# Tile-major residual stream with 16 KB load rows, and rope tables packed as 4 KB rows, in an eight-core diffusion backbone

## The chip, the cores and the metric

One Trainium2 chip, eight cores. Each core computes one sample of the batch; nothing is exchanged between them. The metric is the device time of the slowest core, in microseconds. The kernels fell into a slower state in some executions. In one of the kernel before (3697.43 us), the cores of one die took 3677 to 3696 us at a granted TensorE clock of 0.86 to 0.87, those of the other 3379 to 3394 us at 0.97.

Most fast runs of one kernel agree within about 0.2% (3392.45 to 3398.03 us in nine runs of the kernel before, in one call), and this study is about effects of 0.2 to 0.3%.

## The reference, cut to what matters

Four layers on a stream `x` of 2048 tokens by 1024 channels, with 256 context tokens beside it. Layer 0 begins like this:

```python
mod = silu_c @ w_mod[l] + b_mod[l]                       # shift, scale, gate
hx = modulate(rms_norm(x, norm1_g[l]), sh1, sc1)          # needs x and the modulation
px = hx @ w_in                                            # pooling channels, q, k, v
q = axial_rope(q, ang_r, ang_c); k = axial_rope(k, ang_r, ang_c)
...                                                       # window attention, pooling, MLP
```

The stream is kept transposed: channels on the 128 partitions (8 chunks of 128), tokens along the free dimension, in five tiles: four of 512 latent tokens and one of 256 context tokens.

## The kernel before: the parts that matter

The stream `X` stays in SBUF for the whole run. It is loaded once, tile by tile, on the SyncE queue. In HBM a tile is already one contiguous block of 16 KB for each partition. In SBUF it is chunk-major (all tokens of a chunk lie together, so the eight chunks of one tile lie apart), and the load moves 128 x 8 rows of 2 KB:

```python
X = SB("X", [128, 8, NT], F32)                            # NT = 2304 tokens
def load_x(tile, after=()):
    (t0, n, s, ti) = tile
    Sd.dma("sp", Sd.chan("x%d" % ti), X[:, :, t0:t0 + n],
           xP[:, 8 * t0:8 * (t0 + n)].rearrange("p (c t) -> p c t", c=8), reads=after, writes=xk(ti))
```

`after` names weight slabs: X tile 1 is issued when the third `w_mod` slab has landed, tiles 2 to 4 when the fourth has. Between them the SyncE queue issues the rope tables, two DMAs of 2 KB rows for each tile.

Weights come on another queue, that of GpSimd, which casts float32 in HBM to bfloat16 in SBUF: a slab of 128 rows, 16 KB read and 8 KB written each (`w_kv` is half as wide: 8 KB read and 4 KB written). In the trace their packets have the size written: 8192 and 4096 B. There are four slots. The queue's order at the start is: four `w_mod` slabs, three small constants, then `w_kv`, `w_q`, `w_u` as slots come free, then more `w_mod` slabs:

```python
mods = [get_slab(w_mod[0, j], 8) for j in range(4)]
Sd.dma("pool", Sd.chan("ident"), IDB[:, :], identd, ...)          # rows of 64 B
first_mixer = even_mixer(0, X5, [... load_x(X5[i + 1], [mods[min(i + 2, 3)][1]]) ...])
#   in even_mixer:  permc (rows of 256 B), masks (rows of 512 B) on the GpSimd queue;
#                   for i in range(4): load_rope(i, i); loads[i]()      on the SyncE queue
for j in range(4):
    mod_slab(0, j, mods[j])                                       # then the norm of tile 0, piece by piece
...
kvs = get_slab(w_kv[i2], 8); qs_ = get_slab(w_q[i2], 8); us_ = get_slab(w_u[i2], 8)
kv_tile(all5[0], kvs, rope_buf(0), 1)                             # first K and V matmuls
```

After these three slabs are placed, one slot is left, and the remaining `w_mod` slabs of layer 0 pass through it one after the other. The sixth slab (the second to go through that slot) is issued once the fifth has been used, so the moment when the load of the sixth `w_mod` slab is issued marks how far the start has come; it is my stage mark.

The softmax here doesn't subtract the row's maximum and nothing guards it: scores larger than these inputs give would overflow.

Of the kernel before, what the change touches and what calls it, by code (L numbers as in the profile page):

```python
# [6 lines left out]
F32 = mybir.dt.float32  # L7
BF16 = mybir.dt.bfloat16
ALU = mybir.AluOpType
AF = mybir.ActivationFunctionType  # L10
# [4 lines left out]
NT = S + L  # L15
# [226 lines left out]
def build():  # L242
# [3 lines left out]
    def din(name, shape):  # L246
        dt_in[name] = nc.dram_tensor(name, list(shape), F32, kind="ExternalInput").ap()
        return dt_in[name]
# [14 lines left out]
    identd = din("ident", [128, 32])  # L263
    bandsd = din("bands", [128, 20 * 128])
    masksd = din("masks", [128, 2 * 128])
    ropec = din("ropec", [128, NT])
    ropes = din("ropes", [128, NT])
    permd = din("permc", [128, 128])
    outP = nc.dram_tensor("outP", [128, 8 * S], F32, kind="ExternalOutput").ap()
    gscr = nc.dram_tensor("gscr", [D, GW], BF16).ap()  # L270
# [1 line left out]
    with ExitStack() as st:  # L272
        def SB(name, shape, dt):
            return st.enter_context(nc.sbuf_tensor(name, shape, dt))

        X = SB("X", [128, 8, NT], F32)
        H = SB("H", [128, 8, NT], BF16)
        WR = [SB("wr%d" % i, [128, 4096], BF16) for i in range(NSLOT)]
        nvec = sum(n for _, n in VEC_LAYOUT)
# [21 lines left out]
        def vec(nm, a, b):  # L301
            return VEC[:, voff[nm] + a: voff[nm] + b]

        def emit(Sd, plan):
            dry = Sd.dry
            A = Arena(ART, ARENA_W, Sd)
            psk = lambda i: ("ps", i)
            hk = lambda ti: [("H", ti, c) for c in range(8)]
            xk = lambda ti: [("X", ti, c) for c in range(8)]

            def ACT(out, in_, func, reads, writes, **kw):
                Sd.op("act", "activation", (out, in_, func), kw, reads, writes)
# [4 lines left out]
            def STT(out, in0, scalar, in1, op0, op1, reads, writes):  # L317
                Sd.op("dve", "scalar_tensor_tensor", (out, in0, scalar, in1, op0, op1), None, reads, writes)
# [65 lines left out]
            ACT(SC[:, :], vec("cvec", 0, 16), AF.Silu, VK, [("c", "sc")])  # L384
            def load_x(tile, after=()):
                (t0, n, s, ti) = tile
                Sd.dma("sp", Sd.chan("x%d" % ti), X[:, :, t0:t0 + n], xP[:, 8 * t0:8 * (t0 + n)].rearrange("p (c t) -> p c t", c=8),
                       reads=after, writes=xk(ti))

            def zero_pads():  # L390
# [30 lines left out]
            def gate(which, c, s):  # L421
                o_ = ((3 * which + 2) * 8 + c) * 2 + s
                return MODV2[cur["lb"]][:, o_:o_ + 1]
# [3 lines left out]

            def norm_sq(tile, c, k=2):
                (t0, n, s, ti) = tile
                ACT(H[:, c:c + k, t0:t0 + n], X[:, c:c + k, t0:t0 + n], AF.Square, [("X", ti, q) for q in range(c, c + k)],  # L430
                    [("H", ti, q) for q in range(c, c + k)])

            def norm_stats(tile, r, pb=None):
# [10 lines left out]
            def norm_piece(lb, nrm, tile, r, c, mode="da"):  # L444
                (t0, n, s, ti) = tile
                tb = c % 2
                rst, rk, ak = RST[:, r, 0:n], ("rst", r), ("ab", lb, nrm, c // 2)
                tmp, x, h = TMP[:, tb, 0:n], X[:, c, t0:t0 + n], H[:, c, t0:t0 + n]
                if mode == "da":
                    STT(tmp, x, abv(lb, nrm, 0, c, s), rst, ALU.mult, ALU.mult, [("X", ti, c), rk, ak], [("tmp", tb)])  # L450
                    ACT(h, tmp, AF.Identity, [("tmp", tb), ak], [("H", ti, c)], bias=abv(lb, nrm, 1, c, s), scale=1.0)
                else:
                    if mode == "pd":
                        Sd.op("pool", "tensor_tensor", (tmp, x, rst, ALU.mult), None, [("X", ti, c), rk], [("tmp", tb)])
                    else:
                        TT(tmp, x, rst, ALU.mult, [("X", ti, c), rk], [("tmp", tb)])
                    DVE("tensor_scalar", (h, tmp, abv(lb, nrm, 0, c, s), abv(lb, nrm, 1, c, s), ALU.mult, ALU.add),
                        [("tmp", tb), ak], [("H", ti, c)])
# [14 lines left out]
            def push_final(tile, outb, sq=True):  # L473
                (t0, n, s, ti) = tile
                ob, ok = outb
                if sq:
                    for c in (0, 2, 4, 6):
                        push((lambda c_: (lambda: norm_sq(tile, c_)))(c))
                r = next_rst()
                push(lambda: norm_stats(tile, r))  # L480

                def piece(c):
                    STT(ob[:, c, 0:n], X[:, c, t0:t0 + n], vec("fing", c, c + 1), RST[:, r, 0:n], ALU.mult, ALU.mult,
                        [("X", ti, c), ("rst", r)] + VK, [ok[c]])
                    if c % 2:
                        Sd.dma("sp", Sd.chan("o%d%d" % (ti % 2, c // 2)), outP[:, 8 * t0 + (c - 1) * n:8 * t0 + (c + 1) * n].rearrange("p (c t) -> p c t", c=2),
                               ob[:, c - 1:c + 1, 0:n], reads=ok[c - 1:c + 1])
                for c in range(8):
                    push((lambda c_: (lambda: piece(c_)))(c))

            def mlp_phase(l, tiles, next_l, next_tiles):
# [24 lines left out]
                def stage2(w2s, it, last):  # L516
                    (t0, n, s, ti) = tiles[it]
                    hb, hbk = hid[it % 2]
                    for oc in range(8):
                        pb = dbank()  # L520
                        for kk in range(4):
                            MM(PS[pb][:, 0:n], w2s[0][:, kk, oc * 128:(oc + 1) * 128], hb[:, kk, 0:n], kk == 0, kk == 3,
                               reads=[w2s[1], hbk[kk]], writes=[psk(pb)], last=(kk == 3))
                        STT(X[:, oc, t0:t0 + n], PS[pb][:, 0:n], gate(1, oc, s), X[:, oc, t0:t0 + n], ALU.mult, ALU.add,
                            [psk(pb), gkey(1, oc), ("X", ti, oc)], [("X", ti, oc)])
                        if last and ti in next_ti and oc % 2:
                            norm_sq(tiles[it], oc - 1)
                        step()
                    if last and ti in next_ti:
                        if is_final:  # L530
                            push_final(tiles[it], outbs[it % 2], sq=False)
                        else:
                            push_norm(next_l % 2, 0, tiles[it], ("n1", ti), NORM1_MODE, sq=False)
# [19 lines left out]
            def proj_item(slabs_, tile, oc):  # L553
                (t0, n, s, ti) = tile
                pb = dbank()
                sl = slabs_[oc // 4]
                for k in range(8):
                    MM(PS[pb][:, 0:n], sl[0][:, k, (oc % 4) * 128:(oc % 4 + 1) * 128], H[:, k, t0:t0 + n], k == 0, k == 7,
                       reads=[sl[1], ("H", ti, k)], writes=[psk(pb)], last=(k == 7))
                STT(X[:, oc, t0:t0 + n], PS[pb][:, 0:n], gate(0, oc, s), X[:, oc, t0:t0 + n], ALU.mult, ALU.add,  # L560
                    [psk(pb), gkey(0, oc), ("X", ti, oc)], [("X", ti, oc)])

            def conv_mixer(l, tiles):
# [164 lines left out]
            def even_mixer(l, tiles, loads=()):  # L728
# [7 lines left out]
                V, Vk0 = A.bf16("V", 18, 128, parts=9)  # L736
                Qs = [A.bf16("Qs%d" % i, 4, 512, parts=4) for i in range(2)]
                Us = [A.bf16("Us%d" % i, 512) for i in range(NU_)]
                Pb = [A.bf16("P%d" % i, 1024) for i in range(NP)]
                Db = [A.bf16("Db%d" % i, 512) for i in range(2)]  # L740
                BND, Bk = A.bf16("BND", 20, 128)
                MSK, Mk = A.bf16("MSK", 2, 128)
                PW, PWk = A.bf16("PW", 4, 128)
                RT = [(A.f32("rc%d" % i, 512), A.f32("rs%d" % i, 512)) for i in range(2)]
                t1, t1k = A.f32("t1", 512)
                UB = [A.bf16("UB%d" % i, 512) for i in range(2)]
                PRM, PRk = A.bf16("PRM", 128)
# [8 lines left out]
                cur["nbank"] = 7  # L756

                def rope_buf(i):
                    if i < 2:
                        return RT[i]  # L760
                    return tuple((Pb[2 * i - 4 + j][0].bitcast(F32), Pb[2 * i - 4 + j][1]) for j in range(2))

                def load_rope(ti, i):
                    t0, n = all5[ti][0:2]
                    (rc, rck), (rs, rsk) = rope_buf(i)
                    Sd.dmas("sp", Sd.chan("rt%d" % i), [(rc[:, 0:n], ropec[:, t0:t0 + n]), (rs[:, 0:n], ropes[:, t0:t0 + n])], writes=rck + rsk)

                def rope_a(pq, tab, n):
                    (rc, rck), (rs, rsk) = tab
                    ub = UB[cnt["u"] % 2]  # L770
                    cnt["u"] += 1
                    TT(t1[:, 0:n], PS[pq][:, 0:n], rc[:, 0:n], ALU.mult, [psk(pq)] + rck, t1k)
                    TT(ub[0][:, 0:n], PS[pq][:, 0:n], rs[:, 0:n], ALU.mult, [psk(pq)] + rsk, ub[1])
                    return ub

                def rope_bc(ub, n, dst, dkeys):
# [312 lines left out]
def _prep_shared(inp):  # L1089
# [50 lines left out]
    sh["ident"] = ident  # L1140
    sh["bands"] = bands
    sh["masks"] = masks
    sh["ropec"] = rc
    sh["ropes"] = rs
    return {k: np.ascontiguousarray(v, dtype=np.float32) for k, v in sh.items()}, vecs

def run(inputs, cores=8):
# [21 lines left out]
```

## Time and profile before

| what | value | view |
|---|---|---|
| time, median of 3 runs | 3395.78 us (3393.93 to 3396.72) | runs |
| profiled run, slowest core | 3394.9 us | page |
| PE busy | 90% | page, part 1 |
| DMA's share of the chain of waits | 4% | page, part 4 |
| DMA share in the first four 20 us windows | 0.89, 1.01, 1.01, 0.99 | windows |

Part 4 of the page follows the work that ended last back to the start and says on which engine each share of the span was spent. Before:

```profile
PE 72%; DVE 13%; ACT 8%; DMA 4%; issue 2%; POOL 0%; SPq 0%; DVEq 0%; POOLq 0%; ACTq 0%
```

The kernel is bound by matmuls; loads hold it for 4% of the span, and a part of that lies at the start. The windows view of the start, with the length of a stretch, the busy us of PE, PEld, DVE, ACT and POOL in it (in brackets their instructions), then the granted clock, the mean busy share of the 16 DMA engines, and the GB/s that they wrote:

```profile
0.00:20.00 20.00, 0.99 (x32) 0.94 (x32) 0.75 (x6) 2.99 (x4) 4.60 (x12) 1.00 0.89 169
20.00:40.00 20.00, 1.24 (x33) 1.07 (x34) 0.50 (x3) 1.76 (x2) 0.53 (x1) 1.00 1.01 200
40.00:60.00 20.00, 13.37 (x115) 7.01 (x115) 10.30 (x21) 9.62 (x13) 0.53 (x1) 1.00 1.01 259
60.00:80.00 20.00, 13.47 (x67) 6.97 (x70) 10.59 (x17) 11.14 (x15) 0.00 (x0) 0.74 0.99 268
```

For 80 us the DMA engines have no pause, and PE is nearly idle for the first 40. The chain of waits in order of time names what it waits for (start, length, what):

```profile
2.75 29.76 DMA wr<-w_mod
32.53 24.18 DMA X<-xP
...
106.99 10.16 DMA wr<-w_mod
118.52 8.62 DMA wr<-w_mod
```

The DMA view of the first 130 us gives, for each load, its size and the time from issue to landing:

```profile
X<-xP SPq DMA_DIRECT2D x4, 2048.0 KB, 28.5
wr<-w_q POOLq DMA_DIRECT2D x1, 1024.0 KB, 27.0
wr<-w_kv POOLq DMA_DIRECT2D x1, 512.0 KB, 27.6
ARENA<-masks POOLq DMA_DIRECT2D x1, 64.0 KB, 38.1
ARENA<-permc POOLq DMA_DIRECT2D x1, 32.0 KB, 37.6
IDB<-ident POOLq DMA_DIRECT2D x1, 8.0 KB, 36.4
```

Even 8 KB take 36 us to land, because they stand in line behind four weight slabs: on the eight cores the first packet of the identity starts at 34.4 to 35.6 us. The timeline of PE shows the first K matmuls of the kernel, and what ended the idle time before them:

```profile
49.95 2.34 PE L144 MATMUL psa<-H,wr 128*128 128x512 bf16 x5 [0.24 <-issue]
53.09 1.03 PE L144 MATMUL psa<-H,wr 128*128 128x512 bf16 x2 [0.80 <-ACT H L144]
```

They proceed as ScalarE and VectorE deliver the normed tile; `w_kv` is already there (issued at 19.4, landed at 47.0 us).

### The profile page before, as it was taken

The numbers are of one execution on the slowest core, as the hardware profiler recorded it, in microseconds if no ns is written. First come the engines' busy times: TensorE is split into PE (matmuls) and PEld (weight loads), VectorE is DVE, ScalarE is ACT, GpSimd is POOL, SyncE is SP. The second block draws the span as 40 slices with busy tenths as digits, with TensorE's granted clock in tenths as the row PEclk, the third lists the DMA queues.
The fourth block names the chain that finished last, engine by engine and source line by source line (L and its number), as shares of the span: only waits on it lengthen the run. The fifth ranks groups of instructions, "written<-read, shape, count | busy, mean of one in ns | idle before, by whom it ended". The sixth has DMA issues, their size and how long they took to land.

```text
span 3394.9 us, 43893 instructions; the slowest of 8 cores (3378.4 to 3394.9 us)
## 1 busy us (share of the span) xinstructions
PE 3041.7 (90%) x17850; PEld 1406.6 (41%) x18180; DVE 1925.0 (57%) x2957; ACT 1153.3 (34%) x1684; POOL 217.3 (6%) x259
## 2 busy tenths in 40 slices
PE   3588899999989879999996888999998988899998
PEld 2333355555444334545543332444443433344443
DVE  3444466666752466666657444666666326666666
ACT  3266631111232575111122466311114147511113
POOL 0000000000230000000005000000004000000000
PEclk9799999999999999999998999999999999999999
DMA  9710123432224622424422101225251362121212
GB/s 220 126 21 1 30 50 58 80 63 53 47 56 100 153 61 50 75 50 75 74 45 36 26 1 27 50 51 99 50 99 31 69 161 76 26 50 33 42 25 99
DMA packets 87914, 215.54 MB, mean 63 GB/s; under 512 B 13344, under 2 KB 61088, under 8 KB 70816
## 3 DMA queue, kind: packets, MB, share of 16 engines
q0 software_dynamic: 21360, 141.25, 23.7%
q1 hardware_dynamic: 66352, 71.47, 7.7%
q8 instruction: 142, 2.33, 0.3%
q14 instruction: 60, 0.49, 0.1%
HBM read 336.36 MB, written 17.56 MB: 104 GB/s over the span
## 4 chain that ended last, share of the span: by engine, by line
PE 72%; DVE 13%; ACT 8%; DMA 4%; issue 2%; POOL 0%; SPq 0%; DVEq 0%; POOLq 0%; ACTq 0%
PE psa L144 72%; DVE ARENA L144 5%; ACT ARENA L144 3%; ACT H L144 3%; DVE H L144 3%; DVE X L144 3%; DMA wr<-w_mod 2%; DVE TMP L144 2%; DMA ARENA<-gscr 1%; DMA X<-xP 1%; ACT L144 1%; ACT RST L144 1%; POOL TMP L144 0%; DMA ARENA<-permc 0%; SPq L144 0%
## 5 line engine op out<-in xcount | busy, mean ns | idle before, releaser
L144 PE MATMUL psa<-H,wr 128*128 128x512 bf16 (+1 forms) x7091 | 1550.8, 372 | 90.2 <-ACT H L144 21.9
L144 ACT ACTIVATE ARENA<-psa 128x512 f32<-128x512 f32 (+3 forms) x895 | 581.6, 654 | 1693.6 <-PE psa L144 1666.8
L144 PEld LDWEIGHTS psa<-H,wr 128*128 128x128 bf16 x7280 | 705.4, 99 | 890.4 <-issue 56.4
L144 PE MATMUL psa<-ARENA,wr 128*128 128x512 bf16 (+1 forms) x4520 | 976.5, 369 | 59.2 <-DVE X L144 53.5
L144 DVE SCALAR_TENSOR_TENSOR X<-psa,MODV,X 128x512 f32<-128x512 f32 (+1 forms) x1296 | 905.5, 718 | 152.9 <-PE psa L144 87.4
L144 DVE TENSOR_TENSOR ARENA<-ARENA 128x512 bf16<-128x512 f32 (+4 forms) x789 | 525.1, 667 | 748.1 <-ACT ARENA L144 745.6
L144 PEld LDWEIGHTS psa<-ARENA,wr 128*128 128x128 bf16 x4608 | 443.5, 98 | 569.5 <-DVE X L144 105.5
L144 PE MATMUL psa<-ARENA 128*32 128x512 bf16 (+5 forms) x3390 | 318.7, 375 | 91.0 <-ACT ARENA L144 49.3
L144 PEld LDWEIGHTS psa<-ARENA 128*32 128x32 bf16 (+3 forms) x3404 | 121.1, 100 | 309.0 <-issue 142.3
L144 DVE TENSOR_TENSOR ARENA<-psa,ARENA 128x512 bf16<-128x512 f32 (+2 forms) x186 | 122.3, 677 | 220.3 <-PE psa L144 192.3
L144 ACT ACTIVATE H<-X 128x1024 bf16<-128x1024 f32 (+1 forms) x164 | 161.1, 1000 | 182.6 <-DVE X L144 144.6
L144 ACT ACTIVATE H<-TMP,AB 128x512 bf16<-128x512 f32 (+1 forms) x164 | 113.2, 697 | 173.9 <-DVE TMP L144 173.9
L144 POOL DMA_DIRECT2D wr<-w x64 | 34.0, 531 | 2031.9 <-PE psa L144 2031.9
L144 POOL TENSOR_TENSOR TMP<-X,RST 128x512 f32<-128x512 f32 (+1 forms) x112 | 140.2, 1258 | 202.5 <-ACT RST L144 152.9
L144 PE MATMUL psa<-H,ONES 128*128 128x512 bf16 (+1 forms) x441 | 115.3, 377 | 29.1 <-ACT H L144 19.8
L144 DVE SCALAR_TENSOR_TENSOR TMP<-X,AB,RST 128x512 f32<-128x512 f32 (+1 forms) x164 | 115.3, 712 | 41.3 <-ACT RST L144 41.1
L144 DVE TENSOR_SCALAR H<-TMP,AB 128x512 bf16<-128x512 f32 (+1 forms) x132 | 125.4, 954 | 10.5 <-POOL TMP L144 9.4
L144 DVE CAST H<-ARENA 128x512 bf16<-128x512 f32 (+1 forms) x72 | 29.7, 413 | 127.1 <-ACT ARENA L144 127.1
L144 PE MATMUL psa<-SC,wr 128*128 128x2 bf16 x1536 | 46.0, 164 | 62.2 <-DMA wr<-w_mod 51.6
L144 PE MATMUL psa<-wr,H 128*128 128x128 bf16 (+1 forms) x552 | 85.4, 314 | 11.0 <-DVE ARENA L144 10.8
L144 PEld LDWEIGHTS psa<-H,ONES 128*128 128x128 bf16 x472 | 42.7, 99 | 91.2 <-ACT H L144 30.6
L144 PEld LDWEIGHTS psa<-SC,wr 128*128 128x128 bf16 x1536 | 44.0, 97 | 71.0 <-issue 45.9
(44 smaller groups left out, 661.8 us busy)
## 6 DMA issues: line engine op xcount, KB each, us to landing
wr<-w POOLq DMA_DIRECT2D x64, 1024.0 KB, 10.4
wr<-w_mod POOLq DMA_DIRECT2D x48, 1024.0 KB, 8.1
ARENA<-gscr SPq DMA_DIRECT2D x256, 135.0 KB, 3.0
wr<-pw POOLq DMA_DIRECT2D x12, 1024.0 KB, 8.9
gscr<-ARENA SPq DMA_DIRECT2D x65, 128.0 KB, 1.7
X<-xP SPq DMA_DIRECT2D x4, 2048.0 KB, 28.5
outP<-ARENA SPq DMA_DIRECT2D x16, 512.0 KB, 2.7
wr<-w_out POOLq DMA_DIRECT2D x4, 1024.0 KB, 10.0
```

The lines of the kernel that those rows point to most:

```text
L144: ins = getattr(e, it[1])(*it[2], **it[3])
```

## The change

The intent is fewer and longer DMA rows. X becomes tile-major in SBUF too (the eight chunks of a tile side by side), so that the load of a tile is 128 rows of 16 KB (8 KB for the context tile). The cosine and sine tables of a tile lie side by side, one DMA of 4 KB rows instead of two of 2 KB. The core of the diff:

```diff
-        X = SB("X", [128, 8, NT], F32)
+        X = SB("X", [128, 8 * NT], F32)
+            xv = lambda t0, n: X[:, 8 * t0:8 * (t0 + n)].rearrange("p (c t) -> p c t", c=8)
...
-  Sd.dma("sp", Sd.chan("x%d" % ti), X[:, :, t0:t0 + n], xP[:, 8 * t0:8 * (t0 + n)].rearrange("p (c t) -> p c t", c=8),
+  Sd.dma("sp", Sd.chan("x%d" % ti), X[:, 8 * t0:8 * (t0 + n)], xP[:, 8 * t0:8 * (t0 + n)],
...     # every X[:, c, t0:t0 + n] becomes xv(t0, n)[:, c, :]
-  Sd.dmas("sp", Sd.chan("rt%d" % i), [(rc[:, 0:n], ropec[:, t0:t0 + n]), (rs[:, 0:n], ropes[:, t0:t0 + n])], writes=rck + rsk)
+  Sd.dma("sp", Sd.chan("rt%d" % i), tab, roped[ti], writes=tk)
```

Bytes moved stay the same.

More of the change, by code (lines that the diff above doesn't have):

```diff
@@ L265, in build @@
     masksd = din("masks", [128, 2 * 128])
-    ropec = din("ropec", [128, NT])
-    ropes = din("ropes", [128, NT])
+    roped = din("rope", [4, 128, 1024])
     permd = din("permc", [128, 128])
@@ L429, in norm_sq @@
                 (t0, n, s, ti) = tile
-                ACT(H[:, c:c + k, t0:t0 + n], X[:, c:c + k, t0:t0 + n], AF.Square, [("X", ti, q) for q in range(c, c + k)],
+                ACT(H[:, c:c + k, t0:t0 + n], xv(t0, n)[:, c:c + k, :], AF.Square, [("X", ti, q) for q in range(c, c + k)],
                     [("H", ti, q) for q in range(c, c + k)])
@@ L447, in norm_piece @@
                 rst, rk, ak = RST[:, r, 0:n], ("rst", r), ("ab", lb, nrm, c // 2)
-                tmp, x, h = TMP[:, tb, 0:n], X[:, c, t0:t0 + n], H[:, c, t0:t0 + n]
+                tmp, x, h = TMP[:, tb, 0:n], xv(t0, n)[:, c, :], H[:, c, t0:t0 + n]
                 if mode == "da":
@@ L482, in piece @@
                 def piece(c):
-                    STT(ob[:, c, 0:n], X[:, c, t0:t0 + n], vec("fing", c, c + 1), RST[:, r, 0:n], ALU.mult, ALU.mult,
+                    STT(ob[:, c, 0:n], xv(t0, n)[:, c, :], vec("fing", c, c + 1), RST[:, r, 0:n], ALU.mult, ALU.mult,
                         [("X", ti, c), ("rst", r)] + VK, [ok[c]])
@@ L523, in stage2 @@
                                reads=[w2s[1], hbk[kk]], writes=[psk(pb)], last=(kk == 3))
-                        STT(X[:, oc, t0:t0 + n], PS[pb][:, 0:n], gate(1, oc, s), X[:, oc, t0:t0 + n], ALU.mult, ALU.add,
+                        STT(xv(t0, n)[:, oc, :], PS[pb][:, 0:n], gate(1, oc, s), xv(t0, n)[:, oc, :], ALU.mult, ALU.add,
                             [psk(pb), gkey(1, oc), ("X", ti, oc)], [("X", ti, oc)])
@@ L559, in proj_item @@
                        reads=[sl[1], ("H", ti, k)], writes=[psk(pb)], last=(k == 7))
-                STT(X[:, oc, t0:t0 + n], PS[pb][:, 0:n], gate(0, oc, s), X[:, oc, t0:t0 + n], ALU.mult, ALU.add,
+                STT(xv(t0, n)[:, oc, :], PS[pb][:, 0:n], gate(0, oc, s), xv(t0, n)[:, oc, :], ALU.mult, ALU.add,
                     [psk(pb), gkey(0, oc), ("X", ti, oc)], [("X", ti, oc)])
@@ L738, in even_mixer @@
                 Us = [A.bf16("Us%d" % i, 512) for i in range(NU_)]
+                po = A.off
                 Pb = [A.bf16("P%d" % i, 1024) for i in range(NP)]
+                PT = [(ART[:, po + 1024 * i:po + 1024 * (i + 1)], Pb[2 * i][1] + Pb[2 * i + 1][1]) for i in range(2)]
                 Db = [A.bf16("Db%d" % i, 512) for i in range(2)]
@@ L743, in even_mixer @@
                 PW, PWk = A.bf16("PW", 4, 128)
-                RT = [(A.f32("rc%d" % i, 512), A.f32("rs%d" % i, 512)) for i in range(2)]
+                RT = [A.f32("rt%d" % i, 1024) for i in range(2)]
                 t1, t1k = A.f32("t1", 512)
@@ L758, in rope_buf @@
                 def rope_buf(i):
-                    if i < 2:
-                        return RT[i]
-                    return tuple((Pb[2 * i - 4 + j][0].bitcast(F32), Pb[2 * i - 4 + j][1]) for j in range(2))
+                    return RT[i] if i < 2 else PT[i - 2]
                 def load_rope(ti, i):
-                    t0, n = all5[ti][0:2]
-                    (rc, rck), (rs, rsk) = rope_buf(i)
-                    Sd.dmas("sp", Sd.chan("rt%d" % i), [(rc[:, 0:n], ropec[:, t0:t0 + n]), (rs[:, 0:n], ropes[:, t0:t0 + n])], writes=rck + rsk)
+                    tab, tk = rope_buf(i)
+                    Sd.dma("sp", Sd.chan("rt%d" % i), tab, roped[ti], writes=tk)
                 def rope_a(pq, tab, n):
-                    (rc, rck), (rs, rsk) = tab
+                    tab, tk = tab
                     ub = UB[cnt["u"] % 2]
                     cnt["u"] += 1
-                    TT(t1[:, 0:n], PS[pq][:, 0:n], rc[:, 0:n], ALU.mult, [psk(pq)] + rck, t1k)
-                    TT(ub[0][:, 0:n], PS[pq][:, 0:n], rs[:, 0:n], ALU.mult, [psk(pq)] + rsk, ub[1])
+                    TT(t1[:, 0:n], PS[pq][:, 0:n], tab[:, 0:n], ALU.mult, [psk(pq)] + tk, t1k)
+                    TT(ub[0][:, 0:n], PS[pq][:, 0:n], tab[:, 512:512 + n], ALU.mult, [psk(pq)] + tk, ub[1])
                     return ub
@@ L1142, in _prep_shared @@
     sh["masks"] = masks
-    sh["ropec"] = rc
-    sh["ropes"] = rs
+    sh["rope"] = np.stack([np.concatenate([r[:, i * 512:(i + 1) * 512] for r in (rc, rs)], axis=1) for i in range(4)])
     return {k: np.ascontiguousarray(v, dtype=np.float32) for k, v in sh.items()}, vecs
```

## The prediction

> **What bounds the kernel now.** The page's chain of waits is PE 72%, DVE 13%, ACT 8%, DMA only 4%; PE is busy 90% of 3394.9 us. The change bears on the first 85 us: the window view shows DMA share 0.89, 1.01, 1.01, 0.99 in the four 20 us windows to 80 us, and the chain there reads 29.8 us for the modulation weights (w_mod), then 24.2 us for X.
>
> **Bandwidth: little to win.** In the packet records a 2 KB X packet takes about 95-100 ns when X loads alone (16 engines: about 335-350 GB/s); a weight packet (16 KB read, 8 KB written after the cast) takes about 0.75 us, again about 340 GB/s read. So rows of 16 KB should take about 0.72-0.75 us each, as many bytes per us. [...] DVE and ACT operands keep their sizes: I expect the same 718 ns (X update) and 1.04 us (square).
>
> **Who gets the bandwidth changes.** [...] from 10 to 34 us each 1 us slice starts about 17 weight packets and 17 X packets. So today X gets 2 KB per weight packet; afterwards a turn is 16 KB. I replayed both orders in a two-queue turn-taking estimate with these packet times; for before it gives landings within 1-5 us of the trace. Estimates, corrected by that offset:
> - X tile 0: 38 -> about 16 us. Useless: its norm also waits for the fourth w_mod slab.
> - Fourth w_mod slab: 38 -> about 42-43 (shares with X tile 1).
> - X tile 1: 56.7 -> about 46; tile 2: 71 -> about 55.
> - The small loads (identity, permutation, masks: 24 tiny packets per engine) now concede a 16 KB turn each, and w_kv stands behind them in the same queue: w_kv 47 -> about 62; w_q 54 -> about 73; w_u 70 -> about 83.
>
> **On the critical path.** Today the first K matmuls run at 50 us, the first V copy at 57.7, q at 75, and the w_mod slab that starts the serial weight chain at 107. With w_kv at 62, the first V copy comes at about 68; from there the order is compute-bound, so the rest shifts by about 10 us. Later rope loads (layer 2) have no waiter.
>
> Predicted time: 3405 us, about 9 us (0.3%) slower; 80% range 3392 to 3414. Chance of faster by over 2%: 0.01; within 2%: 0.98; slower by over 2%: 0.01.
>
> **What would show it.** Right: X packets of 16 KB at about 0.72-0.8 us; X tile 0 landing before 20 us; w_kv landing after 55 us and the first K matmuls waiting for it; the K matmuls of tile 0 about 10 us later. Wrong: w_kv landing by 48, or X rows cut into smaller packets, or durations of the X updates changing.
>
> **What would make it wrong.** If long rows are cut to 2-4 KB packets, weights lose less, and the change could even gain some us; if long rows move clearly faster than 350 GB/s, X and weights both land early, for a gain of 5-8 us. The granted clock (0.97 mean, cores spread 3378 to 3395 us) can move the slowest core by some us either way.

The forecast: `w_kv` 15 us later (47 to 62), of which about 10 us reach the first V copy (57.7 to 68), and about 9 us on 3396 for the total, 3405 us. The turn-taking in it is my estimate from the packet counts that the text gives.

## The result, and the profile after

Before: 3396.72, 3395.78 and 3393.93 us in fast runs, 3434.57 in a slow one. After: 3405.19, 3400.73 and 3406.16 us in fast runs, 3918.66 and 3455.80 in slow ones. The ratio of after to before is 1.0025, with a 95% interval of 1.0002 to 1.0048: slower by a quarter of a percent, far inside the 2% that counts as the same. (A ratio is the mean time of one kernel's fast runs over that of the other's in the same rounds, so it is not quite the ratio of the medians.) A second measurement of the same pair with five rounds, below, gave 1.0025 again, 1.0011 to 1.0040.

Part 4 of the page after the change, first line:

```profile
PE 72%; DVE 13%; ACT 8%; DMA 4%; issue 2%; POOL 0%; SPq 0%; DVEq 0%; POOLq 0%; ACTq 0%
```

In whole per cents nothing has moved; the question is one of a few microseconds. The chain of waits in order of time shows them:

```profile
1.55 17.52 DMA wr<-w_mod
19.21 1.01 PE psa L144 x32
20.50 39.89 DMA wr<-w_kv
60.53 4.99 PE psa L144 x40
...
115.53 10.04 DMA wr<-w_mod
126.95 8.54 DMA wr<-w_mod
```

X has left the early chain. In its place stands `w_kv`, and the sixth `w_mod` slab starts at 115.53 instead of 106.99 us. The DMA view of the first 130 us after the change:

```profile
X<-xP SPq DMA_DIRECT2D x4, 2048.0 KB, 21.1
wr<-w_q POOLq DMA_DIRECT2D x1, 1024.0 KB, 42.1
wr<-w_kv POOLq DMA_DIRECT2D x1, 512.0 KB, 39.9
ARENA<-masks POOLq DMA_DIRECT2D x1, 64.0 KB, 49.3
ARENA<-permc POOLq DMA_DIRECT2D x1, 32.0 KB, 44.6
IDB<-ident POOLq DMA_DIRECT2D x1, 8.0 KB, 42.2
```

X got faster, and everything on the other queue slower. The timeline of PE has the first K matmuls 10.6 us later, and names their releaser:

```profile
60.53 3.19 PE L144 MATMUL psa<-H,wr 128*128 128x512 bf16 x8 [18.70 <-DMA wr<-w_kv]
```

The windows after the change, the same four stretches:

```profile
0.00:20.00 20.00, 0.79 (x30) 0.82 (x31) 0.25 (x3) 6.88 (x8) 4.05 (x11) 1.00 0.90 207
20.00:40.00 20.00, 5.57 (x80) 2.89 (x77) 6.78 (x18) 3.48 (x5) 1.06 (x2) 0.90 1.01 182
40.00:60.00 20.00, 0.99 (x32) 0.94 (x32) 2.63 (x7) 1.78 (x2) 0.53 (x1) 0.50 1.01 256
60.00:80.00 20.00, 12.07 (x66) 5.25 (x67) 9.53 (x16) 9.46 (x12) 0.00 (x0) 0.76 0.93 286
```

The DMA engines are as full as before (shares 0.90, 1.01, 1.01, 0.93), but from 40 to 60 us PE works 0.99 us instead of 13.37: it waits for a slab of half a megabyte.

The stage on all cores, read from the traces (my own table: medians over the 8 cores, us; "landed" is the last of the 16 completion counts that the trace has for each load):

```
                                             before    after
X tile 0 landed                                37.3     15.4
fourth w_mod slab landed                       38.6     40.9
X tile 1 landed                                56.6     45.3
w_kv landed                                    46.5     60.2
w_q landed                                     53.5     71.3
first K matmul                                 48.8     60.4
first V matmul                                 53.0     63.6
sixth w_mod slab's load issued (stage mark)   107.2    114.9
from the stage mark to the end               3277.8   3279.9
span of the core                             3385.6   3394.4
```

The start lost 7.7 us and the rest of the kernel, 3278 to 3280 us, took the same time within its scatter (the eight cores of one profile differ by 11 to 23 us there). The median span grew by 8.8 us.

### The profile page after: what moved, and what is told of

Same layout as the page of the kernel before. It is cut to its first block, busy times and chain, and to the rows that moved or that the text cites. A ratio compares the mean times of both kernels' runs of the same rounds, so it can differ in the third digit from the quotient of the medians.

```text
span 3403.7 us, 44209 instructions; the slowest of 8 cores (3381.5 to 3403.7 us)
## 1 busy us (share of the span) xinstructions
PE 3073.8 (90%) x18180; PEld 1406.7 (41%) x18180; DVE 1925.2 (57%) x2957; ACT 1151.2 (34%) x1684; POOL 216.9 (6%) x259
## 4 chain that ended last, share of the span: by engine, by line
PE 72%; DVE 13%; ACT 8%; DMA 4%; issue 2%; POOL 0%; SPq 0%; DVEq 0%; POOLq 0%; ACTq 0%
PE psa L144 72%; DVE ARENA L144 5%; ACT ARENA L144 3%; ACT H L144 3%; DVE H L144 3%; DVE X L144 3%; DVE TMP L144 2%; DMA wr<-w_mod 2%; DMA wr<-w_kv 1%; DMA ARENA<-gscr 1%; ACT L144 1%; ACT RST L144 1%; POOL TMP L144 0%; DMA ARENA<-permc 0%; SPq L144 0%
## 5 line engine op out<-in xcount | busy, mean ns | idle before, releaser
L144 PE MATMUL psa<-H,wr 128*128 128x512 bf16 (+1 forms) x7280 | 1576.7, 373 | 92.8 <-ACT H L144 21.2
## 6 DMA issues: line engine op xcount, KB each, us to landing
wr<-w POOLq DMA_DIRECT2D x64, 1024.0 KB, 10.6
```

The costliest lines, as they stand in the source:

```text
L144: ins = getattr(e, it[1])(*it[2], **it[3])
```

## The experiments

My theory, T, from packet counts (under "Turns by packet" below): a DMA engine takes turns between the SyncE queue and the GpSimd queue, one packet each, and a packet is one row. By T the change did not speed up the engines; it made X's turn eight times as long (16 KB for 2 KB) and thereby handed X the bandwidth of the weights, of which `w_kv` is the one that everything waits for. Rivals: R1, the packed rope rows do it; R2, the tile-major layout in SBUF costs engine time; R3, it is a matter of order or bandwidth and not of the size of a turn; R4, the small loads ahead of `w_kv` cost by their bytes; R5 and R6 stand with the last runs. All ten kernels run for this gave the reference's output within tolerance.

The table collects the stage on all cores (medians over 8 cores of each profile, us) and the ratio of fast runs to those of the kernel before:

```
run                     X0     w3     w_kv   first K  X1     stage mark   rest     ratio  (95% interval)
                        landed landed landed matmul   landed
before                  37.3   38.6   46.5   48.8     56.6     107.2     3277.8
after                   15.4   40.9   60.2   60.4     45.3     114.9     3279.9   1.0025 (1.0002, 1.0048)
e8_after_again          15.9   41.5   60.8   61.0     47.5     115.9     3276.2   1.0025 (1.0011, 1.0040)
e1_x_only               15.9   41.5   58.8   59.0     48.6     113.5     3279.1   1.0015 (0.9991, 1.0040)
e2_rope_only            38.4   39.0   47.8   49.6     56.6     106.9     3278.7   0.9999 (0.9969, 1.0028)
e3_rows_2k              41.0   36.0   44.7   52.3     57.5     109.1     3280.2   1.0004 (0.9980, 1.0028)
e4_rows_4k              37.4   39.3   51.0   51.1     53.5     105.9     3281.0   0.9990 (0.9947, 1.0033)
e5_small_late           15.8   41.1   51.9   52.3     47.9     106.6     3277.1   1.0003 (0.9990, 1.0016)
e6_before_small_late    37.9   38.8   44.0   49.4     55.8     107.0     3275.0   1.0001 (0.9987, 1.0015)
e7_ordered              12.2   39.6   42.4   42.5     49.9     100.8     3278.6   0.9978 (0.9964, 0.9992)
e9_before_ordered       33.6   39.8   42.6   45.1     51.3     112.8     3274.8   1.0010 (0.9996, 1.0024)
e10_first_long          16.0   40.1   47.3   47.6     56.0     106.4     3277.5   0.9996 (0.9977, 1.0014)
```

("X0", "X1": X tiles 0 and 1; "w3": the fourth `w_mod` slab; "rest": from the stage mark to the end.) The rest stays between 3274.8 and 3281.0 in all of them without following the change: what differs happens before the stage mark. Single totals scatter by some us. Each line is one profile; the two of the changed kernel differ by up to 2.2 us in the columns of the stage, so no difference below about 2 us is read here.

### The yardstick

The changed kernel once more, unaltered.

> The changed kernel unaltered, as a yardstick on the same chip as the next three. All theories: ratio to before 1.002 to 1.003; median over the 8 cores: w_kv lands at 59 to 61 us, the sixth w_mod slab's load starts at 114 to 116 us (107 before).

Measured as expected: 1.0025, `w_kv` at 60.8, stage mark at 115.9 us. The loss is small and repeats.

### One half of the change at a time

For the first kernel the rope part of the diff was taken back; for the second, the X part.

```diff
 # e1_x_only: X as in the change, rope as before
-  Sd.dma("sp", Sd.chan("rt%d" % i), tab, roped[ti], writes=tk)
+  Sd.dmas("sp", Sd.chan("rt%d" % i), [(rc[:, 0:n], ropec[:, t0:t0 + n]), (rs[:, 0:n], ropes[:, t0:t0 + n])], writes=rck + rsk)
 # e2_rope_only: the reverse, X[:, :, t0:t0 + n] and its load as before
```

> X tile-major with rows of 16 KB, rope tables left as pairs of 2 KB rows. Theory T (the DMA engines take turns packet by packet between the SyncE queue and the GpSimd queue, and a turn of X has grown from 2 KB to 16 KB, which delays w_kv behind X): nearly all of the loss stays; w_kv lands at 56 to 60 us (47 before, 59 to 60 with the whole change), first K matmuls at about 58 to 60 us, the sixth w_mod slab's load starts at about 114 us (107 before), total 3400 to 3407 us. Rival R1 (the packed rope rows do it): w_kv at about 47, total as before, 3394 to 3398 us.

> Rope packed as 4 KB rows, X left as before (2 KB rows, chunk-major). Theory T: w_kv lands at 46 to 48 us, first K matmuls at about 50 us, total as before, 3393 to 3398 us. Rival R1 (the packed rope rows cause the loss): w_kv late, total 3402 to 3407 us.

With X alone, `w_kv` lands at 58.8 and the stage mark stands at 113.5, 6.3 of the 7.7 us; its fast runs were 3400.3 to 3404.6 us, as expected, but the interval of the ratio reaches 1. With rope alone, nothing: 47.8, 106.9 us, ratio 0.9999. The chain of waits of the two shows it too. X alone:

```profile
20.23 37.92 DMA wr<-w_kv
...
113.57 10.27 DMA wr<-w_mod
```

Rope alone, where the chain waits for X as before:

```profile
1.50 36.14 DMA X<-xP
106.64 11.05 DMA wr<-w_mod
```

R1 is out as the main cause. Packing the rope does shift one thing clearly: `w_q` landed at 65.8 us with the tables in pairs (64.8 to 66.8 on the eight cores), and at 71.3 and 71.7 in the two profiles of the whole change (69.8 to 73.2). T has a reason that no run isolates: a pair of tables is 256 packets in the trace and a packed one 128, so 16 and 8 for each of the 16 DMA engines if they share them evenly, and the pair concedes eight more turns to the weights before X's long rows come; eight turns of 0.70 us are 5.6 us (worked out). The first Q matmuls come at 82.0 us (median) without the packing and at 82.8 with it, long after `w_q` in both, so they don't wait for it.

### The new layout with short rows, and rows of middle length

Here X is tile-major in SBUF, but lies in HBM as `G` groups of chunks, so that a row is 16 KB / G: 2 KB for G = 8, 4 KB for G = 4.

```diff
-  X[:, 8 * t0:8 * (t0 + n)], xP[:, 8 * t0:8 * (t0 + n)],
+  X[:, 8 * t0:8 * (t0 + n)].rearrange("p (g u) -> p g u", g=G),
+  xP.rearrange("p (g u) -> p g u", g=G)[:, :, (8 // G) * t0:(8 // G) * (t0 + n)],
```

> The whole change, but X lies chunk-major in HBM, so that its load moves rows of 2 KB into the tile-major buffer: the new layout in SBUF with the old packets. Theory T: as before: X packets of 2 KB, w_kv at 46 to 48 us, first K matmuls at about 50 us, total 3393 to 3398 us. Rival R2 (the tile-major layout in SBUF itself costs time on VectorE, ScalarE [...]): the loss stays, total 3402 to 3407 us, and X updates longer than 718 ns.

> As the run with 2 KB rows, but two chunks side by side in HBM: rows of 4 KB. Theory T gives a dose: my turn-taking estimate puts w_kv at 50 us (47 at 2 KB, 59 at 16 KB) and X tile 0 at about 26 us, so first K matmuls at about 51 to 53 us and total 3396 to 3400 us. Rival R3 (the loss depends on tile order or total bandwidth, not on the size of a turn): w_kv at either 47 or 59, not between.

With 2 KB rows `w_kv` is early again, 44.7 us. The updates of X take the same time in all layouts. The groups view, shapes kept apart, for before:

```profile
L144 DVE SCALAR_TENSOR_TENSOR X<-psa,MODV,X 128x512 f32<-128x512 f32 x1152 | 844.0, 748 | 149.1 <-PE psa L144 83.7 <-remote 4.5
```

and for after, where X is tile-major:

```profile
L144 DVE SCALAR_TENSOR_TENSOR X<-psa,MODV,X 128x512 f32<-128x512 f32 x1152 | 843.9, 748 | 149.1 <-PE psa L144 87.9
```

748 ns each (the 718 ns of my prediction is the mean with the 256-token tiles included), and the median over both sizes is 749 or 750 ns in before, after and the runs with 2 and 4 KB rows. R2 is out.

This run was not a pure return to before, though, and part of my expectation failed: the first K matmul came at 52.3 us, not about 50, the stage mark at 109.1, and the totals reached 3399.82, where 3398 was the upper end. `w_kv` was there at 44.7; X tile 0 landed late, at 41.0, and the norm waited for it. In the trace the first weight packet starts at 3.1 us (median of the cores) where X lies group-major in HBM, against 6.7 us before; X lost its head start. Why the weights start earlier in these runs, I have not settled.

Rows of 4 KB put `w_kv` at 51.0, between 44.7 and 60.2, as the turn-taking estimate said (50). X tile 0 landed at 37.4, not at 26, for the same lost head start. So the dose is right for the load that matters (against R3): 44.7, 51.0 and 60.2 us with rows of 2, 4 and 16 KB. The earlier start of the weights is mixed into both of these runs; the last run below has short rows for tiles 1 to 4 without it (first weight packet at 7.3 us, after 7.5), and its `w_kv` lands at 47.3. The stage mark came at 105.9, and the fast runs at 3392.46 to 3395.16, below the 3396 to 3400 that I expected. The first K matmuls with 4 KB rows, still held by `w_kv`:

```profile
51.53 3.57 PE L144 MATMUL psa<-H,wr 128*128 128x512 bf16 x8 [1.92 <-DMA wr<-w_kv]
```

### Small loads out of the way

The identity and the masks are 8 KB and 64 KB, but 128 packets each in the trace (of 64 and 512 B), together 16 for each of the 16 engines if they share them evenly. They are first needed long after `w_kv`; here they are issued behind `w_u`.

```diff
 mods = [get_slab(w_mod[0, j], 8) for j in range(4)]
-Sd.dma("pool", Sd.chan("ident"), IDB[:, :], identd, writes=[("c", "idb")])
 ...                                    # masks likewise taken out of even_mixer for layer 0
 for j in range(4): mod_slab(0, j, mods[j]) ...
+load_masks()
+Sd.dma("pool", Sd.chan("ident"), IDB[:, :], identd, writes=[("c", "idb")])
```

> The changed kernel with two small loads (identity 8 KB, masks 64 KB, together 16 packets per engine) moved behind w_u in the GpSimd queue; the permutation stays. Theory T (each packet in that queue, however small, concedes one X packet of 16 KB): 16 turns of about 0.7 us fewer ahead of w_kv, my estimate has w_kv at about 51 us instead of 60 (every core), the sixth slab's load at about 106 to 109 us, total 3393 to 3399 us. Rival R4 (bytes, not turns: 72 KB are 0.2 us at 340 GB/s): w_kv at 59 to 60, nothing gained.

> The kernel before with the same move. Theory T: the 16 turns concede 2 KB packets of 0.1 us here, so only about 2.5 us of w_kv's landing goes (47 to about 44), and the first K matmuls are then held by X tile 0 (its norm ends at about 49 to 50 us): total within 3 us of before. Rival R4: no change at all.

In the changed kernel this alone takes `w_kv` from 60.8 to 51.9 us, and the ratio from 1.0025 to 1.0003. 72 KB at the 340 GB/s of the prediction are 0.2 us; 16 turns of a 16 KB row at its median of 0.70 us are 11 us (both worked out). Measured: 8.9 us. The first K matmuls, on the profiled core:

```profile
52.30 3.19 PE L144 MATMUL psa<-H,wr 128*128 128x512 bf16 x7 [9.72 <-DMA wr<-w_kv]
```

In the kernel before, the same move brings `w_kv` 2.5 us forward, which gains nothing, because the first K matmuls then wait for the norm of X tile 0. R4 is out.

How unevenly this falls can be read from the 16 completion counts of each load. My own listing for core 4, after the change, in us (each row sorted):

```
ident  36.9 37.0 37.2 37.4 37.5 37.5 37.5 37.5 37.7 37.7 37.7 38.1 38.2 38.4 45.3 46.0
permc  37.2 37.5 37.6 37.7 37.7 37.9 37.9 38.0 38.0 38.0 38.4 38.4 38.6 39.0 47.9 49.0
masks  37.8 37.9 38.0 38.0 38.2 38.3 38.3 38.3 38.4 39.9 40.6 41.1 41.2 42.3 54.0 54.1
w_kv   45.1 45.1 45.7 46.5 46.9 46.9 47.0 47.6 47.7 47.9 48.0 48.2 48.3 48.6 59.8 60.4
```

Fourteen counts of `w_kv` come by 48.6 us, two at 59.8 and 60.4; of its 128 packets 112 start by 47.8 us and 16 from 54.0 us on. The records name no engine. My reading, which they don't show: each count is one engine's; on fourteen the small packets slipped through before the rows of X tile 1 began (first at 37.5 us), and two, a little behind, met those rows. On cores 0, 2, 6 and 7 all sixteen counts are late (53.9 to 60.2 us). Either way the last count of `w_kv` comes at about 60, and the first K matmuls wait for it (60.53 us on core 4).

### Loads in the order of their use

If long rows are not bad in themselves, they should be good where nothing urgent stands beside them. In this kernel the permutation goes first; X tile 1 waits for the fourth `w_mod` slab, tile 2 for `w_kv`, tiles 3 and 4 for `w_q`; `w_q` waits for X tile 1 (which reads the slot that `w_q` will fill, as far as the scheduler knows); identity and masks go behind `w_u`.

```diff
-load_x(X5[i + 1], [mods[min(i + 2, 3)][1]])              # issued all together
+gates = [[1, 3], [0], [1], [1]]                          # slots that must have landed
+load_x(X5[i + 1], [("W", k) for k in gates[i]])          # tiles 2 to 4 emitted after mod_slab 0 to 3
```

> The changed kernel with the loads put in the order of their use: permutation first; X tile 1 waits for the fourth w_mod slab, X tile 2 for w_kv, tiles 3 and 4 for w_q; w_q waits for X tile 1; identity and masks behind w_u. Long rows, but each has its turn where nothing urgent stands beside it. Theory T: w_kv lands at 43 to 46 us, first K matmuls at 44 to 47 us, the sixth slab's load at 99 to 103 us; total 3385 to 3393 us, faster than before by 0.1 to 0.3%. If long rows were bad in themselves (R2) it would stay slower than before.

The first K matmuls start at 42.5 us, even earlier than expected, the stage mark is at 100.8, and the fast runs took 3385.08 to 3389.52 us (median 3388.19), 0.9978 of before with an interval of 0.9964 to 0.9992. It beats both kernels, if only by 0.2%. Its chain of waits, in order of time:

```profile
3.78 36.47 DMA wr<-w_mod
40.27 10.34 DMA X<-xP
...
101.38 8.94 DMA wr<-w_mod
```

### Is it the order alone, and is tile 0 to blame?

The last two kernels are the same order with the kernel before (short rows), and the changed kernel in its own order with only X tile 0 in long rows:

```diff
 # e10_first_long
+if ti == 0: pair = (X[:, 0:4096], xP[:, 0:4096])                                        # rows of 16 KB
+else:       pair = (xv(t0, n), xP[:, 4096:].rearrange("p (c t) -> p c t", c=8)[:, :, t0 - 512:t0 - 512 + n])   # 2 KB
```

> The kernel before (2 KB rows) with the same order of loads as the ordered version: what of that version's gain is the order alone? Theory T: with short rows X tile 0 still trickles in at one 2 KB packet per weight packet and lands at about 37 to 39 us, so its norm holds the first K matmuls until about 48 to 50 us although w_kv has landed at 42 to 45; the sixth slab's load starts at 103 to 108 us (101 in the ordered version with long rows, 107 before); total 3391 to 3397 us. Rival R5 (the order alone makes the gain, long rows are worth nothing): first K matmuls at about 43 us, sixth slab at about 101 us, total 3385 to 3390 us.

> The changed kernel in its own order, but only X tile 0 in rows of 16 KB; tiles 1 to 4 in rows of 2 KB. Theory T: the loss comes from tiles 1 and 2 beside the small loads and w_kv, not from tile 0: w_kv lands at 45 to 48 us, X tile 0 at about 16 us, first K matmuls at 46 to 49 us, the sixth slab's load at 103 to 107 us; total 3390 to 3397 us. Rival R6 (pushing tile 0 ahead of the weights is what delays everything): w_kv near 60 us, total 3402 to 3407 us.

The order alone does not make the gain: with short rows the stage mark comes later than before (112.8; the ratio of 1.0010 has an interval that reaches 1). R5 is out. My own expectation failed in part, though. X tile 0 landed at 33.6 (expected 37 to 39) and the first K matmuls came at 45.1, sooner than I said (48 to 50); the stage mark came later (expected 103 to 108), and two of the four fast runs lie above the expected 3391 to 3397 us (3398.36 and 3403.39). The time was lost after the first K matmuls. Its chain of waits:

```profile
44.18 35.44 DMA X<-xP
...
113.21 9.41 DMA wr<-w_mod
```

X tile 2, issued once `w_kv` had landed, now has `w_q`, `w_u` and the next `w_mod` slab beside it, gets 2 KB for each 16 KB that they read (from 60 to 74 us, 16 to 22 packets of X and 16 to 20 of weights start per us and core), and lands at 78.5 us (median), where the long rows of the ordered version landed at 61.5. It is the same sharing, about one packet for one, with the other side losing.

With only tile 0 in long rows, `w_kv` lands at 47.3 and the first K matmuls start at 47.6, no later than in the kernel before (48.8); the stage mark is 106.4 and the ratio 0.9996:

```profile
49.60 3.19 PE L144 MATMUL psa<-H,wr 128*128 128x512 bf16 x7 [7.10 <-DMA wr<-w_kv]
```

So tile 0 in long rows costs nothing, and the loss came from the long rows of the later tiles. The run changes tiles 1 to 4 together; tiles 1 and 2 are the ones that land beside the small loads and `w_kv` (45.3 and 56.9 us, tile 3 at 75.4). R6 is out.

## Why the prediction was right, point by point

- **Time.** 3405 us predicted, 3400.73, 3405.19 and 3406.16 measured in fast runs; +0.3% predicted, +0.25% measured. Right. That it fits to a few us is partly luck: the stage lost 7.7 us (8.7 in the repeat) where 10 were forecast, and single totals scatter by as much as the difference.
- **No bandwidth to win.** An X tile of 512 tokens is one load of 2 MiB before and after, and its rows of 2 KB already moved 345 GB/s: from 70 to 75 us before, with X and rope rows nearly alone in the engines, a 2 KB packet took 95 ns on average, and 16 x 2048 B / 95 ns = 345 GB/s (worked out for the 16 engines). Over the first 100 us and all cores, a 16 KB row took 0.70 us (median) and 0.81 us (mean), a weight packet with its 16 KB read 0.63 to 0.65 and 0.76 to 0.77 us in both kernels. The 0.72 to 0.8 us that I expected lies between the median and the mean.
- **Turns by packet.** Counted over all cores, 3425 weight packets and 3746 X packets of 2 KB started from 10 to 34 us before; 302 weight packets and 316 X rows of 16 KB from 8 to 12 us after. About one for one in both, so the share of bandwidth went with the row. That a turn was one row is in the spacing of X's packets (last section).
- **Landings.** Predicted and measured medians: X tile 0 16 and 15.4; fourth `w_mod` slab 42 to 43 and 40.9; X tile 1 46 and 45.3; tile 2 55 and 56.9; `w_kv` 62 and 60.2; `w_q` 73 and 71.3; `w_u` 83 and 79.2. All within 4 us in this profile. In the repeat tile 2 landed at 67.0, 12 us later than predicted (and from 53.9 to 69.0 on the cores of the first profile), so the hit on tile 2 is luck; the others stayed within 4 us.
- **Small loads.** Right in effect (8.9 us of `w_kv`'s landing), too general in form: I had all 24 tiny packets of each engine conceding a turn. On the profiled core only two of the sixteen counts of `w_kv` were late, on four of the eight cores all; the last count decides (first K matmuls at 60.53 us, after 60.4).
- **X tile 0 "useless".** Too strong. In the change's order it is nearly so; but the ordered version starts K at 42.5 us with long rows and at 45.1 with short ones.
- **"From there the rest shifts by about 10 us."** The path was right, a size was off. "There" is the first V copy (ScalarE copies the first V out of PSUM). Medians over the cores: first K matmul 48.8 to 60.4 us, first V matmul 53.0 to 63.6, V copy 58.0 to 65.8, stage mark 107.2 to 114.9. So from the V copy on, all shifts alike (7.8 and 7.7 us), as predicted; the V copy itself was put at 68 us and came at 65.8 (67.2 in the repeat), mostly because `w_kv` landed at 60.2 and not at 62. The delay of 11.6 us at the first K matmul shrinks to 7.8 on the way. The first V matmuls end 3.5 us after they start before and 2.2 after. Then, before, the V copy comes 1.5 us after their end: ScalarE sat idle for X tile 1 while the V matmuls ran, and the copy stood behind the squares of that tile (first fence below). After, it follows them at once: the tile had landed (45.3 us) long before the V copy, and nothing there waits for X (second fence). The runs fit this, but none takes that one wait away, and why the V matmuls run faster is not settled.

The timeline before, ScalarE squaring the first chunks of tile 1:

```profile
56.73 1.06 ACT L144 ACTIVATE H<-X 128x1024 bf16<-128x1024 f32 x1 [3.69 <-DMA X<-xP]
```

and after, the remaining chunks of that tile, with the V copy just before them and no wait for X:

```profile
65.54 0.60 ACT L144 ACTIVATE ARENA<-psa 128x512 bf16<-128x512 f32 x1 [15.97 <-PE psa L144]
66.04 2.94 ACT L144 ACTIVATE H<-X 128x1024 bf16<-128x1024 f32 x3
```

What stays open: why the weights' packets start earlier in the two runs with X group-major in HBM (3.1 against 6.7 us), and whether 1.4 us of the stage's loss (114.9 against 113.5) go with the packed rope: `w_kv` landed 1.4 us earlier without it (58.8 against 60.2), but cores of one profile, and two profiles of one kernel, differ by as much.

## What to carry to other kernels

Two full DMA queues shared the engines about packet for packet (3425 weight packets and 3746 X packets), and a packet was a row: `w_kv` landed at 46.5, 51.0 and 60.2 us with rows of 2, 4 and 16 KB in the other queue. So before lengthening rows, ask what waits in the other queue, and whether anything gets faster at all: here rows of 2 KB already moved 345 GB/s. Try long rows where nothing urgent stands beside them (0.9978 of before in the ordered version, 1.0025 in the change's order), and keep tiny constants out of the line in front of a load that the first matmuls need (72 KB moved away brought `w_kv` 8.9 us forward). Read the landing of a load by its last completion count (11 us after the fourteenth of sixteen here), and judge a change of 0.2% by the stage that it touches, on all cores, before you trust the totals.

## What else the traces show of the DMA queues

- A packet in the trace is one row: those of X are of 2048 B before (3746 of them in the count above) and of 16384 B after (316). The counts would be equal with longer turns too, but the starts of X's packets fit turns of one row: before, from 12 to 30 us on all cores, 4221 pairs of X packets start 0.65 to 0.70 us apart, about one weight packet (0.63 us) and one X packet (0.08) together, against 2751 and 2893 pairs in the 50 ns just below and above. Turns of several rows would bunch them at the 84 ns of an X packet instead; there, from 0.05 to 0.10 us, the excess is smaller: 3120 pairs against 2847 and 2814.
- Tiny packets cost `w_kv` more than their bytes (0.2 us for 72 KB, worked out at 340 GB/s): moving 72 KB in 256 packets out of the way brought it 8.9 us forward with 16 KB rows in the other queue, and 2.5 us with 2 KB rows.
- With the engines full, X tile 1, issued at 33.77 us on core 4 after the change, had its first packet start at 37.5 us; over the eight cores the delay was 3.6 to 3.9 us.
- Before the change a rope issue held the SyncE queue for 13.55 us, so that X tile 4 was issued at 70.43 us; after it, such issues took 0.60 to 0.66 us from 34 us on, and tile 4 was issued at 42.92. It goes with X's short rows: up to 14.64 us with the rope alone packed, 0.77 at most with X alone in long rows. What the long issue waits for is not shown. The SyncE timeline before has the line

```profile
56.25 13.55 SPq L144 DMA_DIRECT2D ARENA<-ropec  x1
```

- The 16 completion counts of one load can lie far apart: 11 us (48.6 and 59.8) between the fourteenth and the fifteenth of one load of 512 KB (core 4, after the change).
